# Dense expert ups moved ahead of the last product stage: 39 to 47, with the last six tied behind the one-hot products

## The chip, the cores and the metric

The kernel runs on one core of one Trainium2 chip. The metric is the device time of one execution, in microseconds (us). Three runs of the kernel before gave a median of 1912.57 us (1909.86 to 1913.16). An execution was recorded by the hardware profiler; all durations below come from that record.

The core has engines that run side by side, each in its own fixed order: TensorE (PE in the profile, its weight loads PEld), VectorE (DVE), ScalarE (ACT), GpSimd (POOL) and SyncE (SP), which here only issues DMA transfers. An instruction that waits holds up everything behind it on its own engine.

## The reference, cut to what matters

The block maps `x` of 512 tokens by 1024 features to the same shape: an attention branch and a recurrent branch, merged and added to `x`, and then a retrieval of experts (PEER), the part that matters here:

```python
def peer_ffn(h, w_q, sub_keys, u_tab, v_tab):      # per block of 128 tokens
    q = (hb @ w_q).reshape(PEER_BLOCK, PEER_HEADS, 2, PEER_HALF)
    sc = jnp.einsum('thcd,hcnd->thcn', q, sub_keys)
    s1, i1 = lax.top_k(sc[:, :, 0], 16); s2, i2 = lax.top_k(sc[:, :, 1], 16)
    ...                                            # 16 best of the 256 sums: idx, g = softmax
    act = jax.nn.gelu(jnp.einsum('thkd,td->thk', u_tab[idx], hb))
    return jnp.einsum('thk,thkd->td', g * act, v_tab[idx])
```

Each token picks 16 of 16384 experts in each of 8 heads, 128 picks in all. An expert is one row of `u_tab` and one of `v_tab`, of 1024 floats each.

## The kernel before, in words

The tokens are four blocks of 128. Pass `p0` holds block 0, pass `p1` blocks 1 to 3. The trunk (attention, recurrence, merge, projection) runs for `p0` and then for `p1`. The experts are computed in two ways.

**By gather** (`experts`, blocks 0 and 1): 128 slots, one for each pick. For a slot, POOL issues an indirect DMA (L848) that gathers 128 rows of `uv`, 1 MB, into one of 4 buffers. DVE multiplies the u half with `h2` and sums (L855, tile `uv`), ACT makes the weight `e` (L860, L861), and DVE adds the weighted v half to the running sum (L838, tile `x1g`). Block 0's slots run next to the trunk of `p1`, block 1's next to the dense part below. A gather has a manual dependency on an instruction of the step that it was recorded in, called its turn: in the last stage `turn[0]` is that step's multiplication `o` on DVE (L1028). How many slots a step records is set by `SHARE`: 0.2 for an up next to the search, 0.5 for a group of one-hot products, 0.6 for a product alone, 1.1 for a product with an up.

**Densely** (blocks 2 and 3, 256 tokens): all 16384 experts in 128 chunks of 128.

- *Up* (`up`): the chunk's u rows times the 256 tokens, then a gelu (L917) into a result `y`. The first 39 chunks (`AHEAD`) are made ahead, in plain float32, 8 products of 16 PE instructions in all, from `p1.h2r`, with no work on DVE. The other 89 are made inside the last stage, split in two fp32r terms each: ACT casts (L899), DVE subtracts (L900), and PE does 24 products (tile `st`).
- *Search* (`topk`): DVE finds the picks. `ups_far` puts 26 ups (`LEAD`) on PE next to it (tile `pup`).
- *One-hot products* (`wbuild`): the picks of blocks 2 and 3 become a dense table of weights, 16 groups of 16 tokens. Each group is 16 small products (tile `pw`, L1003), copied by ACT to `wst` and stored to `w_d` in HBM. Here 13 further ups run.
- *Last stage* (`down`): for each chunk DVE multiplies `y` with its weights, read back from `w_d`, into `o` (L1028, three buffers, `OB`), and PE adds `o` times the chunk's v rows to `acc`: 8 instructions of 512 columns. From chunk 24 on an up goes with each product. `run(ex)` at the end takes what slots are left.

The code records instructions in program order; a scheduler with a timeline of its own then sets the order on every engine. So an engine's order need not be the code's. Sync dependencies made with `add_manual_dep` hold in any order.

Of the kernel before, what the change touches and what calls it, by code (L numbers as in the profile page):

```python
# [9 lines left out]
F32 = mybir.dt.float32  # L10
F32R = mybir.dt.float32r
# [4 lines left out]
ALU = mybir.AluOpType  # L16
AX = mybir.AxisListType

P = 128
D = 1024  # L20
KT = D // P
# [41 lines left out]
def block_kernel(  # L63
# [17 lines left out]
    nc = tc.nc  # L81
    V = nc.vector
# [6 lines left out]
    pp = ctx.enter_context(tc.tile_pool(name="pp", bufs=2))  # L89
    dram = ctx.enter_context(tc.tile_pool(name="dram", bufs=1, space=bass.MemoryType.DRAM))  # L90
    wp = ctx.enter_context(tc.tile_pool(name="wp", bufs=4))
    ap = ctx.enter_context(tc.tile_pool(name="ap", bufs=1))
    rg = ctx.enter_context(tc.tile_pool(name="rg", bufs=5))
    trunk = ctx.enter_context(ExitStack())
    s4 = trunk.enter_context(tc.tile_pool(name="s4", bufs=2, side="right"))
    s2 = trunk.enter_context(tc.tile_pool(name="s2", bufs=5, side="right"))

# [107 lines left out]

    def mm(o, lhs, rhs, start, stop):
        terms = [(0, 0)] if len(lhs) == 1 or len(rhs) == 1 else [(0, 0), (0, 1), (1, 0)]
        for i, (a, b) in enumerate(terms):
            nc.tensor.matmul(  # L209
                o, lhs[a], rhs[b], start=start and i == 0, stop=stop and i == len(terms) - 1  # L210
            )


    in_turn = mybir.DependencyInfo(mybir.DependencyClass.Sync, mybir.DependencyReason.SCHED_ONLY)
# [665 lines left out]
    NG = NT2 // TG  # L880
    NCH = SLOTS

    HEAD, MID = 24, 15
    AHEAD = HEAD + MID

    TURN = list(range(HEAD, AHEAD)) + list(range(HEAD)) + list(range(AHEAD, SLOTS))

    LEAD = 26

    WI = 12  # L890

# [9 lines left out]
        return t[:, 0, :], t[:, 1, :]  # L901


    def up(c, S_):
        ks = lambda k: slice(k * P, (k + 1) * P)
        if c < AHEAD:
            u = wp.tile([P, D], F32, tag="raw", name=nm("u"), bufs=3)
            nc.sync.dma_start(u, u_t[c])
            for k in range(KT):
                mm(S_, [u[:, ks(k)]], [p1.h2r[:, k, :]], k == 0, k == KT - 1)  # L910
        else:
            uhi, ulo = chunk(u_t, c, "near")
            for k in range(KT):
                mm(S_, [uhi[:, ks(k)], ulo[:, ks(k)]], [h[:, k, P : 3 * P] for h in p1.h2T], k == 0, k == KT - 1)

    def gelu(o, S_):
        return A.activation(o, S_, AF.Gelu_apprx_tanh)  # L917
# [26 lines left out]


    def kept(c):
        if c >= HEAD:
            return mid.tile([P, NT2], F32, tag="ym", name=nm("y"), bufs=MID)
        if c % WI == 0:
            ybuf.append(rg.tile([P, WI, NT2], F32, tag="r", name=nm("ys")))  # L950
        return ybuf[-1][:, c % WI, :]
# [12 lines left out]
    def dense(ys, kT, kTb, stack):  # L964
# [3 lines left out]
        pt_ = pool("pt", 2, space=PSUM)  # L968
        acc = pa.tile([P, 2, D], F32, tag="acc", name="acc")

        def up_near():
            c = TURN[len(ys)]
            st = pt_.tile([P, 512], F32, tag="st", name=nm("st"))
            up(c, st[:, 0:NT2])
            y = kept(c)
            gelu(y, st[:, 0:NT2])
            ys[c] = y


        def wbuild(tg):  # L980
            o1s = wp.tile([P, TG, P], F32, tag="w8", name=nm("o1s"))
            st = wp.tile([P, NCH, TG], F32, tag="w8", name=nm("wst"))
            for t4 in range(0, TG, 4):
                pw = pt_.tile([P, 4, P], F32, tag="pw", name=nm("pw"))
                t0_ = tg * TG + t4
                o2 = dw.tile([P, 4, P], F32, tag="o2", name=nm("o2"), bufs=4)
                V.tensor_tensor(  # L987
                    o2, iota.unsqueeze(1).to_broadcast([P, 4, P]),
                    kTb[:, t0_ : t0_ + 4].unsqueeze(2).to_broadcast([P, 4, P]), op=ALU.is_equal,
                )  # L990
                for j in range(4):
                    t = t0_ + j
                    o1 = o1s[:, t4 + j, :]
                    k1, g1 = kT[:, 0, 0, t : t + 1], kT[:, 0, 1, t : t + 1]
                    if O1[j] == "A":

                        sq = dw.tile([P, P], F32, tag="osq", name=nm("osq"), bufs=2)
                        A.activation(sq, iota, AF.Square, bias=kT[:, 1, 0, t : t + 1])
                        A.activation(o1, sq, AF.Relu, scale=kT[:, 1, 1, t : t + 1], bias=g1)
                    else:  # L1000
                        e = nc.gpsimd if O1[j] == "P" else V
                        e.tensor_scalar(o1, iota, k1, g1, op0=ALU.is_equal, op1=ALU.mult)  # L1002
                    nc.tensor.matmul(pw[:, j, :], o2[:, j, :], o1, start=True, stop=True)  # L1003
                turn[0] = A.copy(st[:, :, t4 : t4 + 4], pw.rearrange("p t i -> p i t"))  # L1004
            nc.sync.dma_start(w_d[tg], st)

        ws, vs = [], []

# [24 lines left out]
                    mm(acc[:, b, hs], [o[:, bs]], [v_[:, hs]], c == 0, c == NCH - 1)  # L1033

        for tg in range(NG):
            wbuild(tg)
            share("w")
            if len(ys) < AHEAD - 6:
                up_near()

            if tg == 7:
                wtile()
                wload(0, 0, 8)
            elif tg == 13:
                wload(0, 8, 14)
        wload(0, 14, NG)
        while len(ys) < AHEAD:
            up_near()
        for c in range(NCH):
            down(c, ys[c])  # L1050
            if c >= HEAD and len(ys) < NCH:
# [9 lines left out]
    st = {}  # L1061
# [10 lines left out]
    p1.rnn()  # L1072
    p1.merge()
    p1.project()
    trunk.close()
    mid = ctx.enter_context(tc.tile_pool(name="mid", bufs=1, reuse_waits="tile", side="right"))
    run(p1.keys())
    when = []
    for name, mark in marks:
        owed[0] += PACE[name]  # L1080
# [12 lines left out]
        yield from experts(P, x1, h2, (p1.idx[:, 0, :], p1.g[:, 0, :]), lambda s: turn[0], True)  # L1093

    ex = second()
    ys = ups_far(0, LEAD)
    p1.weights()
    kTs = picks_t()
# [86 lines left out]
```

## Time and profile before

| what | value |
|---|---|
| median of three runs | 1912.57 us |
| the profiled execution | 1909.11 us, of which the traced span is 1907.2 us |
| PE busy | 1750.3 us, 92% of the span |
| DVE busy | 1310.4 us, 69% |
| ACT busy, POOL busy | 783.9 us, 41%; 486.7 us, 26% |
| search with ups | 942 to 1050 us of the span |
| one-hot products | 1052 to 1180 us |
| last stage | 1200 to 1901 us |

A busy share is an average over stages, so each stage has to be read by itself: which engine has no gaps there, and what ended the gaps of the others. Names in the trace are tile names of the program without their numbers; "out<-in" says what an instruction writes and reads. A value in square brackets behind a row is the idle time before it and what ended it.

### The profile page before, as it was taken

The page shows a single profiled execution, that of the slowest core. Times are in us where ns is not written, and L with a number is a line of the kernel's source. Part 1 is how long each engine was busy: PE and PEld are TensorE (multiplying, and loading weights), DVE is VectorE, ACT ScalarE, POOL GpSimd, SP SyncE. Part 2 cuts the span into 40 slices and gives each one's busy share as a digit, 9 for nine tenths or more (in the row PEclk, how much of TensorE's full clock was granted, in tenths as well). Part 3 has the DMA queues.
Part 4 walks back from the last instruction along what each step waited for, and adds up shares of the span by engine and source line. Part 5 has one row for each costly group of instructions (what it writes and reads, how often), then busy time and mean ns, then how long its engine had stood idle before and what let it go on. Part 6 is the DMA issues. An engine that isn't in the chain of part 4 may idle for free.

```text
span 1907.2 us, 25762 instructions
## 1 busy us (share of the span) xinstructions
PE 1750.3 (92%) x9166; PEld 1378.6 (72%) x9166; DVE 1310.4 (69%) x2818; ACT 783.9 (41%) x2193; POOL 486.7 (26%) x375
## 2 busy tenths in 40 slices
PE   7899898888798899989996985899999999999998
PEld 6789797778598677779985885347766767667763
DVE  2251387988889987689999567456666666666662
ACT  3382333767678754355311565012222322232220
POOL 1100001545322233342001466122222232222220
PEclk9899897889599899999998998899999999999999
DMA  7488454887877899987464577999999999999893
GB/s 296 149 279 309 172 193 162 297 293 283 308 274 278 313 389 357 386 305 271 155 216 157 177 275 290 362 372 395 366 369 392 382 354 364 354 356 354 331 359 123
DMA packets 131471, 563.37 MB, mean 295 GB/s; under 512 B 11408, under 2 KB 43280, under 8 KB 88592
## 3 DMA queue, kind: packets, MB, share of 16 engines
q1 hardware_dynamic: 94480, 293.29, 42.8%
q0 software_dynamic: 36864, 268.45, 37.0%
q8 instruction: 72, 1.18, 0.2%
q14 instruction: 55, 0.45, 0.1%
HBM read 539.68 MB, written 22.02 MB: 295 GB/s over the span
## 4 chain that ended last, share of the span: by engine, by line
PE 71%; DVE 11%; DMA 9%; ACT 5%; issue 3%; POOL 1%; DVEq 0%; SPq 0%; ACTq 0%; POOLq 0%
PE acc L209 22%; PE st L209 16%; DMA uv<-in_uv_dram,idx 6%; PE ppq L209 5%; PE pkq L209 5%; PE pgt L209 4%; PE pbR L684 4%; PE pbA L677 3%; PE pwo L711 2%; DVE x1f L838 2%; PE pw L1003 2%; PE pvv L209 1%; DMA w_d<-wst 1%; DVE uv L855 1%; DMA v<-in_v_t_dram 1%
## 5 line engine op out<-in xcount | busy, mean ns | idle before, releaser
L848 POOL DMA_INDIRECT uv<-in_uv_dram,idx x256 | 360.4, 1408 | 1075.8 <-DVE x1g L838 284.3
L209 PE MATMUL acc<-v,o 128*128 128x512 f32 x1024 | 449.9, 595 | 22.2 <-DVE o L1028 19.6
L209 PEld LDWEIGHTS acc<-v,o 128*128 128x128 f32 x1024 | 191.8, 191 | 246.5 <-issue 223.3
L209 PE MATMUL st<-a,t 128*128 128x256 f32 x2136 | 282.2, 292 | 0.0
L209 PEld LDWEIGHTS st<-a,t 128*128 128x128 f32 x2136 | 262.5, 191 | 22.2 <-issue 18.9
L838 DVE SCALAR_TENSOR_TENSOR x1g<-uv,e,x1g 128x1024 f32<-128x1024 f32 x128 | 164.3, 1283 | 52.8 <-ACT e L861 52.8
L838 DVE SCALAR_TENSOR_TENSOR x1f<-uv,e,x1f 128x1024 f32<-128x1024 f32 x128 | 164.0, 1281 | 24.9 <-ACT e L870 24.8
L855 DVE SCALAR_TENSOR_TENSOR uv<-uv,h2f 128x1024 f32<-128x1024 f32 x128 | 156.0, 1220 | 34.5 <-DMA uv<-in_uv_dram,idx 27.9
L855 DVE SCALAR_TENSOR_TENSOR uv<-uv,h2g 128x1024 f32<-128x1024 f32 x128 | 155.9, 1218 | 19.4 <-DMA uv<-in_uv_dram,idx 19.4
L860 ACT ACTIVATE e<-e 128x1 f32<-128x1 f32 x128 | 25.8, 202 | 333.7 <-DVE uv L855 333.4
L900 DVE TENSOR_TENSOR t<-raw,t 128x1024 fp32r<-128x1024 f32 x89 | 108.9, 1223 | 68.7 <-ACT t L899 68.7
L1028 DVE TENSOR_TENSOR o<-y,w 128x256 f32<-128x256 f32 x104 | 44.0, 424 | 102.9 <-PE acc L209 102.9
L917 ACT ACTIVATE y<-st 128x256 f32<-128x256 f32 x89 | 34.2, 384 | 193.5 <-PE st L209 193.5
L230 DVE TENSOR_TENSOR wl<-raw,wh 128x1024 fp32r<-128x1024 f32 x76 | 90.8, 1218 | 19.0 <-ACT wh L229 7.3
L899 ACT CAST t<-raw 128x1024 fp32r<-128x1024 f32 x89 | 92.0, 1033 | 23.4 <-PE acc L209 23.4
L229 ACT CAST wh<-raw 128x1024 fp32r<-128x1024 f32 x76 | 76.7, 1046 | 35.0 <-PE pwo L711 12.3
L209 PE MATMUL pup<-r,u 128*128 128x256 f32 x416 | 90.4, 379 | 0.1
L209 PEld LDWEIGHTS pup<-r,u 128*128 128x128 f32 x416 | 78.8, 190 | 11.1 <-issue 0.5
L1003 PE MATMUL pw<-o1s,o 128*128 128x128 f32 x512 | 70.8, 295 | 15.0 <-DVE o L987 9.8
L1002 POOL TENSOR_SCALAR o1s<-iota,r 128x128 f32<-128x128 bf16 x64 | 74.2, 1168 | 38.3 <-ACT r L928 16.3
L1003 PEld LDWEIGHTS pw<-o1s,o 128*128 128x128 f32 x512 | 66.6, 206 | 20.0 <-ACT wst L1004 9.0
L209 PE MATMUL pkq<-wh,a 128*128 128x256 f32 x384 | 78.5, 298 | 0.0
(264 smaller groups left out, 3251.1 us busy)
## 6 DMA issues: line engine op xcount, KB each, us to landing
v<-in_v_t_dram SPq DMA_DIRECT2D x64, 1024.0 KB
raw<-in_u_t_dram SPq DMA_DIRECT2D x89, 512.0 KB
u<-in_u_t_dram SPq DMA_DIRECT2D x39, 512.0 KB
w<-in_w_br_dram SPq DMA_DIRECT2D x16, 1024.0 KB
w_d<-wst SPq DMA_DIRECT2D x16, 1024.0 KB
w<-w_d SPq DMA_DIRECT2D x9, 1536.0 KB
w<-in_w_qkv_dram SPq DMA_DIRECT2D x12, 1024.0 KB
raw<-in_w_qkv_dram SPq DMA_DIRECT2D x24, 512.0 KB
```

The source lines that it names most:

```text
L209: nc.tensor.matmul(o, lhs[a], rhs[b], start=start and i == 0, stop=stop and i == len(terms) - 1)
L229: A.copy(hi[:, i : i + 1024], raw)
L230: V.tensor_tensor(lo[:, i : i + 1024], raw, hi[:, i : i + 1024].bitcast(F32), op=ALU.subtract)
L677: nc.tensor.matmul(pb[:, 0:NT], w.raw(k * P, (k + 1) * P), self.aT[:, k, :], start=(k == 0), stop=(k == H - 1))
L684: nc.tensor.matmul(pb[:, 0:NT], w.raw(1024 + k * P, 1024 + (k + 1) * P), self.rnn_out(k, 1)[:, 0, :], start=(k == 0), stop=(k == NF - 1),)
L838: V.scalar_tensor_tensor(x1, v_, e_, x1, op0=ALU.mult, op1=ALU.add)
L848: i = nc.gpsimd.indirect_dma_start(out=t, out_offset=None, in_=uv, in_offset=bass.IndirectOffsetOnAxis(ap=idx[:, s : s + 1], axis=0),)
L855: i = V.scalar_tensor_tensor(t[:, 0:D], t[:, 0:D], 1.0, h2, op0=ALU.mult, op1=ALU.mult, accum_out=d)
L899: A.copy(t[:, 0, :], raw)
L900: V.tensor_tensor(t[:, 1, :], raw, t[:, 0, :].bitcast(F32), op=ALU.subtract)
L1002: e.tensor_scalar(o1, iota, k1, g1, op0=ALU.is_equal, op1=ALU.mult)
L1003: nc.tensor.matmul(pw[:, j, :], o2[:, j, :], o1, start=True, stop=True)
```

## The change

It makes 47 ups ahead in place of 39, and 81 in the last stage in place of 89. Of the 47, 31 are recorded next to the search (26 before), 10 between the one-hot products (7 before), and 6 behind them, as before. New is that the first product of each of these six has a dependency on the last one-hot product, so that the scheduler cannot put them earlier. The eight more results lie in a tile `spare`, and two tiles `h2s` hold the split token operand for the ups of the last stage, made by one cast on ACT and one subtraction on DVE. Both take the place in SBUF of the keys' operand buffer (pool `ap`), which is now freed with the trunk, after the keys. The share per step is untouched; the sums of the shares shift since there are fewer steps with an up.

```diff
-    ap = ctx.enter_context(tc.tile_pool(name="ap", bufs=1))
...
+    ap = trunk.enter_context(tc.tile_pool(name="ap", bufs=1, side="right"))
...
-    HEAD, MID = 24, 15
-    AHEAD = HEAD + MID
+    HEAD, MID, SPARE = 24, 15, 8
+    AHEAD = HEAD + MID + SPARE
-    LEAD = 26
+    LEAD, HELD = 31, 6
...
-    def up(c, S_):
+    def up(c, S_, after=None):
...
-                mm(S_, [u[:, ks(k)]], [p1.h2r[:, k, :]], k == 0, k == KT - 1)
+                i = mm(S_, [u[:, ks(k)]], [p1.h2r[:, k, :]], k == 0, k == KT - 1)
+                if after is not None and k == 0:
+                    tc.add_manual_dep(i.ins, after.ins.name, in_turn, reason="in turn")
...
-                mm(S_, [uhi[:, ks(k)], ulo[:, ks(k)]], [h[:, k, P : 3 * P] for h in p1.h2T], k == 0, k == KT - 1)
+                mm(S_, [uhi[:, ks(k)], ulo[:, ks(k)]], [h[:, k, :] for h in h2s], k == 0, k == KT - 1)
...
-            if len(ys) < AHEAD - 6:
+            if len(ys) < AHEAD - HELD:
                 up_near()
...
         while len(ys) < AHEAD:
-            up_near()
+            up_near(last)
+
+        A.copy(h2s[0], p1.h2r)
+        V.tensor_tensor(h2s[1], p1.h2r, h2s[0].bitcast(F32), op=ALU.subtract)
...
+    run(p1.keys())
     trunk.close()
     mid = ctx.enter_context(tc.tile_pool(name="mid", bufs=1, reuse_waits="tile", side="right"))
-    run(p1.keys())
...
+    h2s = [mid.tile([P, KT, NT2], F32R, tag=f"h{i}", name=f"h2s{i}") for i in range(2)]
+    spare = mid.tile([P, SPARE, NT2], F32, tag="spare", name="spare")
```

What the scheduler makes of it shows in the order on the engines. First PE, where the one-hot products (`pw`) end and the last stage (`acc`) begins; `x4` counts products, `st` is an up. Before:

```order
L1003 MATMUL pw_10354<-o1s_10338,o_2090_10355 128x128 x4
L1003 MATMUL pw_10368<-o1s_10338,o_2093_10369 128x128 x4
L1003 MATMUL pw_10382<-o1s_10338,o_2096_10383 128x128 x4
L209 MATMUL acc<-v_10479,o_10481 128x512 x4
L209 MATMUL acc<-v_10479,o_10487 128x512 x4
L209 MATMUL acc<-v_10500,o_10502 128x512 x4
```

And now, at the same place on PE:

```order
L1011 MATMUL pw_10475<-o1s_10445,o_2111_10476 128x128 x4
L1011 MATMUL pw_10489<-o1s_10445,o_2114_10490 128x128 x4
L209 MATMUL st_10512<-r_6202,u_10513 128x256 x8
L209 MATMUL st_10524<-r_6202,u_10525 128x256 x8
L209 MATMUL st_10536<-r_6202,u_10537 128x256 x8
L209 MATMUL st_10548<-r_6202,u_10549 128x256 x8
L209 MATMUL st_10560<-r_6202,u_10561 128x256 x8
L209 MATMUL acc<-v_10588,o_10590 128x512 x3
L209 MATMUL st_10572<-r_6202,u_10573 128x256 x8
L209 MATMUL acc<-v_10588,o_10590 128x512
```

Five of the six tied ups stand between the last one-hot product and the first product of the last stage, the sixth inside that first product.

Second DVE, in the middle of the last stage, around products 59 to 64. The last number in a name grows in the order in which the code records; so a slot `uv` belongs to the `o` whose number is next below its own, and that `o` is its gather's turn. Before:

```order
L1028 TENSOR_TENSOR o_2452_12392<-y_2339_11723,w_2271_11308 128x256
L900 TENSOR_TENSOR t_2455_12401<-raw_2454_12399,t_2455_12401 128x1024
L838 SCALAR_TENSOR_TENSOR x1g_8972<-uv_2433_12286,e_2434_12288,x1g_8972 128x1024
L855 SCALAR_TENSOR_TENSOR uv_2440_12331,e_2441_12333<-uv_2440_12331,h2g_8973 128x1024
L1028 TENSOR_TENSOR o_2461_12441<-y_2346_11768,w_2366_11876 128x256
L838 SCALAR_TENSOR_TENSOR x1g_8972<-uv_2440_12331,e_2441_12333,x1g_8972 128x1024
L900 TENSOR_TENSOR t_2464_12450<-raw_2463_12448,t_2464_12450 128x1024
L855 SCALAR_TENSOR_TENSOR uv_2442_12338,e_2443_12340<-uv_2442_12338,h2g_8973 128x1024
L1028 TENSOR_TENSOR o_2468_12486<-y_2354_11815,w_2366_11876 128x256
L838 SCALAR_TENSOR_TENSOR x1g_8972<-uv_2442_12338,e_2443_12340,x1g_8972 128x1024
L855 SCALAR_TENSOR_TENSOR uv_2450_12385,e_2451_12387<-uv_2450_12385,h2g_8973 128x1024
L1028 TENSOR_TENSOR o_2476_12533<-y_2361_11860,w_2366_11876 128x256
```

Now, in the same stretch on DVE:

```order
L1037 TENSOR_TENSOR o_2486_12595<-y_2312_11556,w_2384_11985 128x256
L1037 TENSOR_TENSOR o_2494_12642<-y_2319_11601,w_2384_11985 128x256
L904 TENSOR_TENSOR t_2466_12465<-raw_2465_12463,t_2466_12465 128x1024
L858 SCALAR_TENSOR_TENSOR uv_2491_12633,e_2492_12635<-uv_2491_12633,h2g_8977 128x1024
L904 TENSOR_TENSOR t_2473_12510<-raw_2472_12508,t_2473_12510 128x1024
L841 SCALAR_TENSOR_TENSOR x1g_8976<-uv_2491_12633,e_2492_12635,x1g_8976 128x1024
L858 SCALAR_TENSOR_TENSOR uv_2499_12680,e_2500_12682<-uv_2499_12680,h2g_8977 128x1024
L841 SCALAR_TENSOR_TENSOR x1g_8976<-uv_2499_12680,e_2500_12682,x1g_8976 128x1024
L1037 TENSOR_TENSOR o_2501_12687<-y_2327_11648,w_2384_11985 128x256
L1037 TENSOR_TENSOR o_2509_12734<-y_2334_11693,w_2384_11985 128x256
```

Before, the slot uv_2450 (turn: the `o` ahead of o_2452) stood behind three more multiplications, o_2452, o_2461 and o_2468. Now two `o` stand together, and the two slots behind them, uv_2491 (turn o_2486) and uv_2499 (turn o_2494), have their turns one and none back. From slot 52 on (product 45) all slots up to 121 stand so, in place of two or three `o` back before; every tenth product has a third slot in its pair.

## Rows read from the trace of the kernel before

**Rows 1.** Stretches: length, busy PE, PEld, DVE, ACT, POOL; PEclk, DMA share, GB/s.
```profile
310.00:540.00 230.00, 195.71 (x1152) 169.88 (x1153) 192.58 (x302) 148.47 (x503) 98.92 (x65) 0.81 0.76 277
540.00:660.00 120.00, 106.41 (x517) 94.26 (x516) 116.49 (x163) 99.64 (x249) 29.94 (x23) 0.94 0.86 308
1200.00:1300.00 100.00, 97.44 (x254) 45.88 (x255) 48.66 (x73) 10.82 (x31) 22.05 (x17) 0.98 1.02 380
1300.00:1500.00 200.00, 200.00 (x1024) 139.92 (x1023) 136.58 (x173) 59.48 (x139) 49.26 (x36) 1.00 0.98 379
```
**Rows 2.** Chain that ended last, in order of time, inside the last stage.
```profile
1350.88 5.75 PE st L209 x48
1356.63 6.87 PE acc L209 x16
```
**Rows 3.** Groups of the last stage: busy, mean ns | idle before, releasers.
```profile
L209 PE MATMUL acc<-v,o 128*128 128x512 f32 x1024 | 449.9, 595 | 22.2 <-DVE o L1028 19.6 <-DMA v<-in_v_t_dram 2.6
L848 POOL DMA_INDIRECT uv<-in_uv_dram,idx x115 | 163.7, 1424 | 512.0 <-DVE x1g L838 284.3 <-DVE o L1028 222.5 <-issue 5.2
L855 DVE SCALAR_TENSOR_TENSOR uv<-uv,h2g 128x1024 f32<-128x1024 f32 x115 | 140.1, 1218 | 0.0
L900 DVE TENSOR_TENSOR t<-raw,t 128x1024 fp32r<-128x1024 f32 x89 | 108.9, 1223 | 68.7 <-ACT t L899 68.7
```
**Rows 4.** Groups of the search: the ups beside it.
```profile
L209 PE MATMUL pup<-r,u 128*128 128x256 f32 x416 | 90.4, 379 | 0.1
```
**Rows 5.** Timeline at the search's end: start, us, engine, line [idle before].
```profile
1044.55 0.87 PE L925 MATMUL pt<-ident,r 128*128 128x128 f32 x3 [12.81 <-DVE r L320]
1050.69 0.90 PE L925 MATMUL pt<-ident,r 128*128 128x128 f32 x3 [5.27 <-DVE r L320]
```
**Rows 6.** Timeline of PE over the one-hot products.
```profile
1051.87 3.37 PE L1003 MATMUL pw<-o1s,o 128*128 128x128 f32 x16 [0.27 <-DVE o L987]
...
1116.60 3.19 PE L209 MATMUL st<-r,u 128*128 128x256 f32 x14
1119.62 8.76 PE L1003 MATMUL pw<-o1s,o 128*128 128x128 f32 x64
...
1173.91 6.41 PE L1003 MATMUL pw<-o1s,o 128*128 128x128 f32 x40 [1.26 <-ACT wst L1004]
1199.94 5.26 PE L209 MATMUL acc<-v,o 128*128 128x512 f32 x6 [19.62 <-DVE o L1028]
```
**Rows 7.** Timeline of the last gather, its turn and its slot.
```profile
1856.01 0.43 DVE L1028 TENSOR_TENSOR o<-y,w 128x256 f32<-128x256 f32 x1 [3.01 <-PE acc L209]
1856.70 1.67 POOL L848 DMA_INDIRECT uv<-in_uv_dram,idx  x1 [2.50 <-DVE o L1028]
...
1870.08 1.22 DVE L855 SCALAR_TENSOR_TENSOR uv<-uv,h2g 128x1024 f32<-128x1024 f32 x1
1871.91 1.28 DVE L838 SCALAR_TENSOR_TENSOR x1g<-uv,e,x1g 128x1024 f32<-128x1024 f32 x1 [0.60 <-ACT e L861]
1873.18 0.43 DVE L1028 TENSOR_TENSOR o<-y,w 128x256 f32<-128x256 f32 x1
```
**Rows 8.** Two gathers issued together, and the slots that waited for them.
```profile
346.57 1.45 POOL L848 DMA_INDIRECT uv<-in_uv_dram,idx  x1 [0.20 <-DVE x1f L838]
348.32 1.99 POOL L848 DMA_INDIRECT uv<-in_uv_dram,idx  x1 [0.30 <-DVE r L465]
...
352.63 1.22 DVE L855 SCALAR_TENSOR_TENSOR uv<-uv,h2f 128x1024 f32<-128x1024 f32 x1 [0.86 <-DMA uv<-in_uv_dram,idx]
355.92 1.23 DVE L855 SCALAR_TENSOR_TENSOR uv<-uv,h2f 128x1024 f32<-128x1024 f32 x1 [0.52 <-DMA uv<-in_uv_dram,idx]
```
**Rows 9.** Chain in order of time: two more gathers that were waited for.
```profile
513.34 6.48 DMA uv<-in_uv_dram,idx
1135.59 10.94 DMA uv<-in_uv_dram,idx
```
**Rows 10.** Waits of DVE: for what, us in total, times, longest us.
```profile
DVE uv L855 <- DMA uv<-in_uv_dram,idx: 47.3, 33, 9.4
```

More of the change, by code (lines that the diff above doesn't have):

```diff
@@ L207, in mm @@
         terms = [(0, 0)] if len(lhs) == 1 or len(rhs) == 1 else [(0, 0), (0, 1), (1, 0)]
-        for i, (a, b) in enumerate(terms):
+        made = [
             nc.tensor.matmul(
@@ L211, in mm @@
             )
+            for i, (a, b) in enumerate(terms)
+        ]
+        return made[0]
     in_turn = mybir.DependencyInfo(mybir.DependencyClass.Sync, mybir.DependencyReason.SCHED_ONLY)
@@ L946, in kept @@
     def kept(c):
+        if HEAD + MID <= c < AHEAD:
+            return spare[:, c - HEAD - MID, :]
         if c >= HEAD:
@@ L969, in dense, with up_near @@
         acc = pa.tile([P, 2, D], F32, tag="acc", name="acc")
-        def up_near():
+        def up_near(after=None):
             c = TURN[len(ys)]
             st = pt_.tile([P, 512], F32, tag="st", name=nm("st"))
-            up(c, st[:, 0:NT2])
+            up(c, st[:, 0:NT2], after)
             y = kept(c)
@@ L1002, in wbuild @@
                         e.tensor_scalar(o1, iota, k1, g1, op0=ALU.is_equal, op1=ALU.mult)
-                    nc.tensor.matmul(pw[:, j, :], o2[:, j, :], o1, start=True, stop=True)
+                    last = nc.tensor.matmul(pw[:, j, :], o2[:, j, :], o1, start=True, stop=True)
                 turn[0] = A.copy(st[:, :, t4 : t4 + 4], pw.rearrange("p t i -> p i t"))
             nc.sync.dma_start(w_d[tg], st)
+            return last
         ws, vs = [], []
@@ L1035, in dense @@
         for tg in range(NG):
-            wbuild(tg)
+            last = wbuild(tg)
             share("w")
-            if len(ys) < AHEAD - 6:
+            if len(ys) < AHEAD - HELD:
                 up_near()
```

## The prediction

> **What bounds the kernel now.** I read the busy times by stage first, then the chain that ended last, then the waits and the timeline at the places that the change touches.
>
> In the last stage PE has no gap: 200.00 us busy of 200.00 at full granted clock [rows 1]. The chain agrees: two ups take 5.75 us, two products 6.87 us, and so on to the end [rows 2]. A near up is thus 2.87 us, a product 3.43 us, and a pair of each 12.62 us. DMA runs close behind, at a share of 0.98 and 379 GB/s [rows 1], but PE waited only 2.6 us for v in the whole stage, and the slots' first DVE step (L855) not at all for its gather: 0.0 idle before its 115 instructions [rows 3]. In the search DVE is the bound; PE ends its 26 ups (90.4 us, 3.48 each) [rows 4] and then idles 12.81 and 5.27 us [rows 5]. Over the one-hot products PE is full while ups stand between them, up to 1119.62; the rest takes until 1180.32, and then PE idles 19.62 us for the stores to `w_d` and their way back [rows 6].
>
> So what PE does in the last stage counts in full, and what it does beside the search or in that gap should cost little. What can turn this round is whatever makes PE wait in the last stage: `o` from DVE.
>
> **Ups taken out of the last stage.** 89 become 81: 8 x 2.87 = 23.0 us less. Their casts (ACT) and subtractions (DVE, 1.22 us each [rows 3]) go too, but neither engine bounds this stage now.
>
> **Ups put in ahead.** Five more beside the search are 5 x 3.48 = 17.4 us, and the idle there is 12.81 + 5.27 = 18.1 us: hidden, though without that cover they would cost all of it. The subtraction for `h2s` covers 2048 elements, two of the 1.22 us kind, 2.44 us on DVE, which bounds the search; between 0 and 2.44 I take the upper end. Between the one-hot products there are 10 ups in place of 13. Before, 1051.87 to 1119.62 held 13 ups (45.2 us) and 96 one-hot products (the other 22.5 us, 0.235 each), and the remaining 160 took 60.7 us, 0.38 each [rows 6]. Now 64 stand among the ups and 192 follow: 10 x 3.48 + 64 x 0.235 + 192 x 0.38 = 123 us for 128 before, so the last one is about 5.6 - 2.4 = 3.2 us earlier. Five tied ups (17.4 us) fit the gap of 19.62 us. The sixth stands inside the first product: 3.5 us in full. Three u loads and three raw loads, 3.1 MB, now come when the last stage starts, where DMA already has a share of 1.02 at 380 GB/s [rows 1]: between 0 and 3.1 MB / 380 GB/s = 8 us; I take 0, since PE's wait for v there was 2.6 us in all and the sixth up gives v 3.5 us more. Sum of this paragraph: about 0, between -4 and +10.
>
> **The new order on DVE.** This is the term that decides. A gather waits for its turn, the `o` of its step. The trace shows it: `o` at 1856.01 (product 117, counted back from the last), gather at 1856.70, 0.69 us later, released by that `o`; its slot began at 1870.08, 13.4 us after the gather, four `o` on [rows 7]. In the middle of the stage the slots stood two or three `o` behind their turn, two to three times 6.3 us, and none waited [rows 3]. Now from product 45 to 104 two `o` come together and the two slots of these turns follow at once. DVE must stand and wait for a transfer that the `o` just ahead of it has released.
>
> How long does a gather take from issue to use? Where a slot waited for it, the row gives it: 352.63 - 346.57 = 6.06 us for the first of two issued 1.75 us apart, 355.92 - 348.32 = 7.60 for the second [rows 8]; single ones 6.48 and 10.94 [rows 9]. DVE had 33 such waits in all [rows 10]; these rows hold the shortest and, to 0.02 us, the longest. In the last stage two are issued together beside v and raw loads, so I take 8.0, and keep 6.1 and 10.9 as bounds.
>
> By the Trainium skill, "DMA: Bandwidth & Descriptors", section "Anatomy of one DMA — SWDGE (gpsimd) path", a DMA from GpSimd takes about 2.0 us and its bytes at 436 GB/s: an estimate of 4.4 us for 1 MB. The rows do not agree: the shortest is 6.06 us, with other transfers on the same engines. By the page's figure a pair would take 7.4 + 4.4 = 11.8 us, under PE's 12.62, and the wait would be hidden.
>
> A pair's cycle on DVE, from the first `o` to the next first `o`: 0.69 us to the gather, 8.0 to land, then slot A 1.2, a subtraction 1.2, x1g of A 1.2, slot B to its x1g 1.83, x1g to the next `o` 1.27 (both from rows 7: 1870.08, 1871.91, 1873.18) [rows 7]. The second gather is issued about 1.75 us after the first, and lands while A is worked on. The sum is 7.4 + 8.0 = 15.4 us, against 12.62 on PE: 2.8 us more for each of 30 pairs, 84 us. Six of these pairs hold a third slot, another 1.2 + 1.2 less 0.6 of the wait for `e` that it fills: 6 x 1.8 = 11 us. Against it stands a lead: with three buffers `o` may be ahead by two products and two pairs of ups, 2 x 3.43 + 4 x 2.87 = 18 us, which DVE loses before PE feels anything.
>
> After product 104 PE has only products left. Five slots there stand none or one `o` behind their turn, and each costs 0.69 + 8.0 + 1.83 + 1.27 + 0.4 = 12.2 us in a row, 61 us for products 104 to 111 and the last two ups, which take PE 8 x 3.43 + 5.75 = 33 us: 28 more. The next three are two `o` behind and cost nothing; three more, one behind, take 10.3 us (no x1g in the chain) for two products of 6.87: 10 more. Together 38.
>
> **Sum.** -23 + 0 + 84 + 11 - 18 + 38 = +92 us. The profiled execution took 1909.1 us (its span and 1.9 around it), 3.5 below the median, which I leave out: 2001, and I predict 2000 us. At 6.1 us for a gather the terms are 13.5 a pair, 26 + 11 - 18 + 23 - 23 = +19, 1928. At 10.9 us 18.3 a pair, 170 + 11 - 18 + 61 - 23 = +201, 2110.
>
> **Rivals.**
>
> *The gathers land in time.* If a gather took 5.2 us or less, the pair would stay at 12.62, the tail would lose little, and what is left is the 23 us: 1909 - 23 = 1886, faster. For it: PE-bound now, five of six ups in a true gap, and with DVE waiting fewer bytes are in flight. Against it: not one waited gather below 6.06 us, with DMA at 277 or 308 GB/s [rows 1, 8, 9], and a pair of 15.4 us still asks 379 x 12.62 / 15.4 = 311 GB/s. The point from which it decides is 5.2 us; at 5.6 or so gain and loss cancel, and the time is as before.
>
> *DMA gets worse in bursts.* The two gathers (2 MB), a v load and raw loads are now released within a few us of each other and then DMA drains. That speaks for 10 us and more for each: 2075 to 2110. Against it: DVE's wait lowers the mean rate, and the second of a pair took 7.60 us [rows 8].
>
> *PE's clock falls in the gaps.* PE would be busy 12.62 of 15.4 us, 82%; from 310 to 540, at 85%, the granted clock was 0.81 [rows 1]. A pair would then take PE 12.62 / 0.81 = 15.6 us, just over DVE's 15.4: some 30 x 0.2 = 6 us more, 2007. It hides behind the same wait and hardly moves the sum.
>
> *The ups don't fill the gap.* If the late u loads or the stores to `w_d` hold each other up, the first product comes up to 10 us later: 2010, inside the range. By the order they are in place.
>
> **Chances.** The DVE wait at 6.1 us and above, up to some 9.5: 0.73; longer gathers: 0.15; the gathers in time: 0.09; gain and loss about equal: 0.03. About 0.2%, 4 us, is what can be told from no change here. Slower 0.88, same 0.03, faster 0.09. The range from 1915 to 2075 leaves out the faster case and the worst of the bursts, a tenth at either end; 1930 to 2050 is the likeliest case's own.
>
> **What would show it.** Right: in the last stage L855's rows (now L858) wait for `uv<-in_uv_dram,idx`, 2 to 5 us each from product 45 on; POOL's gathers are released by `o` in nearly every step; PE's products wait for `o`; the pair of products and ups comes every 15 us in the chain; GB/s there falls to about 310; the first product starts near 1197 us, with five ups in the gap before it. Wrong: slots still without a wait, a gather used 5 us after issue, or the last stage at 12.6 us a pair. If the pair takes 13 or 18 us, the mechanism holds and the gather's time was mis-sized.

## The result, and the profile after

The changed kernel takes 2215.18 us (median of four runs, 2211.71 to 2220.13), the kernel before 1911.21 in the same comparison: a ratio of 1.159, 95% interval 1.156 to 1.162. Slower was forecast, but 2000 us and at most 2075. The loss is more than three times the forecast one (304 us by the medians, where the sum gave 92), and its mechanism is another, so that even the direction came out right for the wrong reason.

First, where the time is. The rows of `o` give it: product 45, product 105 and the last product. The kernel before:

```profile
1410.56 0.42 DVE L1028 TENSOR_TENSOR o<-y,w 128x256 f32<-128x256 f32 x1 [0.86 <-PE acc L209]
...
1788.96 0.42 DVE L1028 TENSOR_TENSOR o<-y,w 128x256 f32<-128x256 f32 x1 [0.86 <-PE acc L209]
...
1890.34 0.43 DVE L1028 TENSOR_TENSOR o<-y,w 128x256 f32<-128x256 f32 x1 [3.01 <-PE acc L209]
```

The same three products of the changed kernel:

```profile
1408.35 0.42 DVE L1037 TENSOR_TENSOR o<-spare,w 128x256 f32<-128x256 f32 x1
...
2094.29 0.42 DVE L1037 TENSOR_TENSOR o<-y,w 128x256 f32<-128x256 f32 x1 [8.92 <-PE acc L209]
...
2201.48 0.42 DVE L1037 TENSOR_TENSOR o<-y,w 128x256 f32<-128x256 f32 x1 [2.72 <-PE acc L209]
```

Up to product 45 the new kernel is 2.2 us ahead. From there to product 105, 30 pairs, it takes 685.9 us in place of 378.4, so 22.9 us a pair in place of 12.6. That is 307.5 of the 311 us. The last 22 products take 107.2 us and took 101.4.

Second, which engine has gaps there. Two stretches of the last stage after (length, busy PE, PEld, DVE, ACT, POOL; PEclk, DMA share, GB/s), the first to be read against the last of [rows 1]:

```profile
1300.00:1500.00 200.00, 161.59 (x743) 105.66 (x742) 117.83 (x149) 46.52 (x111) 39.27 (x30) 0.90 0.81 309
1500.00:1700.00 200.00, 127.35 (x557) 82.31 (x556) 77.39 (x95) 34.15 (x75) 17.80 (x19) 0.79 0.57 206
```

PE had no gap in that stretch before. Now it is idle for more than a third of the second stretch, its granted clock is 0.79, and the DMA share is 0.57. No engine is the bound any more, so the stage is a loop of waits. The groups say what is waited for (busy, mean ns | idle before, releasers):

```profile
L209 PE MATMUL acc<-v,o 128*128 128x512 f32 x1024 | 523.8, 674 | 256.0 <-DMA v<-in_v_t_dram 256.0
L1037 DVE TENSOR_TENSOR o<-y,w 128x256 f32<-128x256 f32 x96 | 40.8, 425 | 390.3 <-PE acc L209 390.3
L858 DVE SCALAR_TENSOR_TENSOR uv<-uv,h2g 128x1024 f32<-128x1024 f32 x128 | 156.5, 1222 | 94.4 <-DMA uv<-in_uv_dram,idx 94.0
L923 ACT ACTIVATE y<-st 128x256 f32<-128x256 f32 x81 | 30.8, 381 | 364.5 <-DVE o L1037 333.3
```

The last of these groups in the kernel before:

```profile
L917 ACT ACTIVATE y<-st 128x256 f32<-128x256 f32 x89 | 34.2, 384 | 193.5 <-PE st L209 193.5
```

Against [rows 3], PE's wait for v grew from 2.6 to 256.0 us. The wait of DVE for gathers, on which the prediction rests, is the smallest of the four (94.0 us, of which 77.8 lie in the last stage). The Gelus have a releaser that they did not have before: there those of the last stage waited for their own sums on PE (193.5 us), never for an `o`.

Third, one pair in order of time (start, us, engine, line [idle before]; `...` stands for rows left out; a row "x2" merges two and runs from the start of the first to the end of the last; SPq is SyncE's queue, on which DMA transfers are issued):

```profile
1519.73 0.43 DVE L1037 TENSOR_TENSOR o<-y,w 128x256 f32<-128x256 f32 x1 [9.54 <-PE acc L209]
...
1520.19 0.38 ACT L923 ACTIVATE y<-st 128x256 f32<-128x256 f32 x1 [11.32 <-DVE o L1037]
...
1520.43 0.94 POOL L851 DMA_INDIRECT uv<-in_uv_dram,idx  x1 [19.11 <-DVE o L1037]
...
1522.56 6.21 PE L209 MATMUL st<-h2s,t 128*128 128x256 f32 x48
...
1523.16 1.05 ACT L903 CAST t<-raw 128x1024 fp32r<-128x1024 f32 x1 [2.59 <-PE acc L209]
...
1525.50 3.29 SPq L901 DMA_DIRECT2D raw<-in_u_t_dram  x2
...
1526.06 1.22 DVE L858 SCALAR_TENSOR_TENSOR uv<-uv,h2g 128x1024 f32<-128x1024 f32 x1 [0.59 <-DMA uv<-in_uv_dram,idx]
...
1527.21 1.22 DVE L904 TENSOR_TENSOR t<-raw,t 128x1024 fp32r<-128x1024 f32 x1
...
1528.88 0.39 SPq L1033 DMA_DIRECT2D v<-in_v_t_dram  x1
...
1536.77 8.79 PE L209 MATMUL acc<-v,o 128*128 128x512 f32 x13 [8.00 <-DMA v<-in_v_t_dram]
...
1543.45 0.42 DVE L1037 TENSOR_TENSOR o<-y,w 128x256 f32<-128x256 f32 x1 [10.80 <-PE acc L209]
```

Read it as a loop. The `o` at 1519.73 releases the Gelu (0.46 us later). The two ups (`st`) then run right behind the products, and end at 1522.56 + 6.21 = 1528.77. Only 0.11 us later is v issued for the next two products. PE can use it 7.9 us after that and stands idle until then; the first products then run at half the clock; and only they let the next `o` be made. A pair is products, ups and a whole v load, one after the other. (Two loads of u stand ahead of v on the queue, and they are out at 1525.50 + 3.29 = 1528.79. So this trace alone doesn't say whether v waits for them or for the ups; experiments 9 and 15 do.)

In the kernel before v went out much earlier, for a pair in the middle 18.2 us before the product that uses it (1577.96 and 1596.12), with the ups and products of the pair ahead still to come on PE:

```profile
1577.96 1.22 SPq L1024 DMA_DIRECT2D v<-in_v_t_dram  x1
```
```profile
1596.12 7.03 PE L209 MATMUL acc<-v,o 128*128 128x512 f32 x16
```

Over the pairs from product 48 to 103 the median is 18.2 us before and 7.7 now.

Counted over the last stage, the `o` at 1519.73 is that of product 55, and the Gelu it releases is that of chunk 70. The same count for all 81: the first 15 Gelus inside the last stage come 20 to 23 products ahead, every later one (from chunk 62, near product 47) exactly 15. Fifteen is the number of buffers that near results take in turn (`MID`). In the kernel before the count was mostly 13 or 14 (12 to 15), and no Gelu waited for an `o`.

Why it binds now is in the code. The ups inside the last stage start at product 24 with the first chunk not made ahead: 39 before, so 15 steps ahead of use, 47 now, so 23 ahead. But the eight `spare` places serve once, for chunks 39 to 46, and all later results share the 15 others. So a near up is recorded eight steps before a buffer for its result can be free.

Last, the stretch between the one-hot products and the first product, which answers to [rows 6]:

```profile
1171.66 2.96 PE L1011 MATMUL pw<-o1s,o 128*128 128x128 f32 x24 [1.28 <-DVE o L995]
1174.46 10.53 PE L209 MATMUL st<-r,u 128*128 128x256 f32 x48
1192.85 9.68 PE L209 MATMUL st<-r,u 128*128 128x256 f32 x32 [7.86 <-DMA u<-in_u_t_dram]
1202.36 2.74 PE L209 MATMUL acc<-v,o 128*128 128x512 f32 x6
```

The gap of 19.62 us before the first product is mostly filled, but PE waits 7.86 us inside it for the u of a tied up. The first product comes 2.4 us later than before; forecast was 3 us earlier.

### The profile page after: what moved, and what is told of

Read it like the earlier page. It is cut to its first block, busy times and chain, and to the rows that moved or that the text cites. A ratio compares the mean times of both kernels' runs of the same rounds, so it can differ in the third digit from the quotient of the medians.

```text
span 2218.3 us, 25677 instructions
## 1 busy us (share of the span) xinstructions
PE 1825.7 (82%) x9102; PEld 1399.2 (63%) x9102; DVE 1313.5 (59%) x2811; ACT 789.1 (36%) x2188; POOL 448.7 (20%) x375
## 4 chain that ended last, share of the span: by engine, by line
issue 40%; PE 31%; DVE 9%; DMA 8%; POOL 8%; ACT 4%; POOLq 0%; DVEq 0%; SPq 0%; ACTq 0%
POOL uv L851 7%; PE acc L209 6%; DMA uv<-in_uv_dram,idx 5%; PE ppq L209 4%; PE pkq L209 4%; PE st L209 3%; DMA v<-in_v_t_dram 2%; PE pry L209 2%; PE prx L209 2%; PE pup L209 1%; PE pvv L209 1%; PE pw L1011 1%; DVE x1f L841 1%; PE pgt L209 1%; DVE uv L858 1%
## 5 line engine op out<-in xcount | busy, mean ns | idle before, releaser
L209 PE MATMUL acc<-v,o 128*128 128x512 f32 x1024 | 523.8, 674 | 256.0 <-DMA v<-in_v_t_dram 256.0
L851 POOL DMA_INDIRECT uv<-in_uv_dram,idx x256 | 317.0, 1238 | 1459.7 <-DVE o L1037 781.4
L209 PEld LDWEIGHTS acc<-v,o 128*128 128x128 f32 x1024 | 219.1, 219 | 531.8 <-issue 278.1
L209 PE MATMUL st<-h2s,t 128*128 128x256 f32 x1944 | 252.4, 288 | 0.0
L209 PEld LDWEIGHTS st<-h2s,t 128*128 128x128 f32 x1944 | 234.3, 188 | 20.4 <-issue 20.1
L858 DVE SCALAR_TENSOR_TENSOR uv<-uv,h2g 128x1024 f32<-128x1024 f32 x128 | 156.5, 1222 | 94.4 <-DMA uv<-in_uv_dram,idx 94.0
L841 DVE SCALAR_TENSOR_TENSOR x1f<-uv,e,x1f 128x1024 f32<-128x1024 f32 x128 | 163.8, 1280 | 22.9 <-ACT e L873 22.8
L903 ACT CAST t<-raw 128x1024 fp32r<-128x1024 f32 x81 | 84.9, 1048 | 146.9 <-PE acc L209 98.9
L904 DVE TENSOR_TENSOR t<-raw,t 128x1024 fp32r<-128x1024 f32 x81 | 99.1, 1224 | 43.4 <-ACT t L903 43.2
L209 PE MATMUL pup<-r,u 128*128 128x256 f32 x496 | 107.9, 379 | 1.5 <-DMA u<-in_u_t_dram 1.5
L209 PEld LDWEIGHTS pup<-r,u 128*128 128x128 f32 x496 | 93.8, 190 | 14.9 <-issue 2.4
L233 DVE TENSOR_TENSOR wl<-raw,wh 128x1024 fp32r<-128x1024 f32 x76 | 90.7, 1217 | 18.3 <-ACT wh L232 6.6
L1010 POOL TENSOR_SCALAR o1s<-iota,r 128x128 f32<-128x128 bf16 x64 | 79.8, 1255 | 20.5 <-PE pw L1011 7.9
L209 PE MATMUL pgt<-a,wh 128*128 128x384 f32 x256 | 70.9, 357 | 5.1 <-DVE r L627 5.1
```

The lines of the kernel that those rows point to most:

```text
L209: nc.tensor.matmul(o, lhs[a], rhs[b], start=start and i == 0, stop=stop and i == len(terms) - 1)
L233: V.tensor_tensor(lo[:, i : i + 1024], raw, hi[:, i : i + 1024].bitcast(F32), op=ALU.subtract)
L841: V.scalar_tensor_tensor(x1, v_, e_, x1, op0=ALU.mult, op1=ALU.add)
L851: i = nc.gpsimd.indirect_dma_start(out=t, out_offset=None, in_=uv, in_offset=bass.IndirectOffsetOnAxis(ap=idx[:, s : s + 1], axis=0),)
L858: i = V.scalar_tensor_tensor(t[:, 0:D], t[:, 0:D], 1.0, h2, op0=ALU.mult, op1=ALU.mult, accum_out=d)
L903: A.copy(t[:, 0, :], raw)
```

## The experiments

Theories: **G**, the prediction's (DVE waits for gathers asked for late); **R** (the ring of 15 buffers); **S** (v stands on SyncE's queue behind loads of u); **T** (the tie, the copied operands or the 47 themselves). **W** came later: v waits for one of four weight buffers.

**1. All 23 buffers in one rotation.**

```diff
     def kept(c):
-        if HEAD + MID <= c < AHEAD:
-            return spare[:, c - HEAD - MID, :]
         if c >= HEAD:
-            return mid.tile([P, NT2], F32, tag="ym", name=nm("y"), bufs=MID)
+            return mid.tile([P, NT2], F32, tag="ym", name=nm("y"), bufs=MID + SPARE)
...
-    spare = mid.tile([P, SPARE, NT2], F32, tag="spare", name="spare")
```

> Still 47 ahead, but the near up products' results take 23 buffers in rotation (the 15 and the eight spare ones together) instead of 15. In the changed kernel an up product is written 23 steps ahead of its use but its result's buffer is freed only 15 steps ahead, so that its Gelu waits for an o (333.3 us over 34 waits on ScalarE, none before). Theory R (the ring of 15): with 23 buffers no Gelu waits for an o, the pair of products takes about 12.6 us again instead of 23.7, and the kernel takes 1888 us (1875 to 1905). Rival T (the tied products, the copied operands or the 47 themselves cost the time): 2215 us as now, within 15.

Measured: 1885.77 us, ratio to before 0.988 (0.985 to 0.991). The stretch of the last stage and the groups of that kernel:

```profile
1500.00:1700.00 200.00, 200.00 (x1023) 138.76 (x1023) 133.35 (x170) 57.64 (x134) 47.84 (x35) 1.00 0.95 363
```
```profile
L209 PE MATMUL acc<-v,o 128*128 128x512 f32 x1024 | 446.9, 592 | 2.0 <-DMA v<-in_v_t_dram 2.0
L858 DVE SCALAR_TENSOR_TENSOR uv<-uv,h2g 128x1024 f32<-128x1024 f32 x114 | 138.9, 1218 | 15.8 <-DMA uv<-in_uv_dram,idx 15.8
L923 ACT ACTIVATE y<-st 128x256 f32<-128x256 f32 x81 | 31.0, 383 | 152.9 <-PE st L209 152.8
```

No Gelu waits for an `o` (they come 20 to 23 products ahead to the end), PE is full at full clock, and on DVE the slots stand two or three `o` behind their turns again. R holds, T falls; the order on DVE was itself a result of the ring.

**2. The near ups begin eight steps later**, with 15 buffers and the spare ones as they were.

```diff
-            if c >= HEAD and len(ys) < NCH:
+            if c >= HEAD + SPARE and len(ys) < NCH:
                 up_near()
-            share("both" if c >= HEAD and len(ys) < NCH else "down")
+            share("both" if c >= HEAD + SPARE and len(ys) < NCH else "down")
```

> Still 47 ahead with 15 buffers and the eight spare ones, but the near up products begin eight steps later, at product 32 instead of 24, so that each is written 15 steps ahead of its use, as in the kernel before. Theory R: no Gelu waits for an o, 12.6 us a pair, 1888 us (1875 to 1905). Rival T: 2215 us within 15.

Measured: 1887.41 us, ratio 0.989 (0.986 to 0.991), and again no Gelu waits for an `o`. It is not the number of buffers but the number against the lead.

**3. No gathers in the last stage.** `for s in range(14 if table else SLOTS)` in `experts`: this leaves out 114 of the 128 slots of block 1, so its outputs are not computed.

> The changed kernel with the second block's slots left out from the fifteenth on (114 gathers, their turns on VectorE and their sums; these outputs are not computed), so no gather runs beside the last stage. Theory G, the prediction's (VectorE waits for gathers that are asked for late): without them the pair falls to 13 us or less and the kernel takes under 1920 us. Theories R and S (S: the v load stands on SyncE's queue behind the loads of u, which wait for VectorE's subtractions, and so comes 8 us late): the Gelu's wait for an o and PE's wait for v stay, the pair takes 18 us or more, and the kernel over 2040 us.

Measured: 2137.74 us, 20.5 us a pair (median between products, as in all that follow). The loop in its bare form:

```profile
1522.31 6.22 PE L209 MATMUL st<-h2s,t 128*128 128x256 f32 x48
...
1528.56 0.38 SPq L1033 DMA_DIRECT2D v<-in_v_t_dram  x1
...
1534.30 9.02 PE L209 MATMUL acc<-v,o 128*128 128x512 f32 x16 [5.77 <-DMA v<-in_v_t_dram]
```

G falls: without one gather beside it the pair still takes 20.5 us of 23.4. v is issued at the end of the ups (1522.31 + 6.22 = 1528.53). What the gathers add is mostly v's landing: from its issue to PE's use of it the median is 7.7 us beside them and 5.9 alone.

**4. Each v load written one pair earlier in the code.**

```diff
             if c % 2 == 0:
-                vs.append(wp.tile([P, 2, D], F32, tag="w8", name=nm("v")))
-                nc.sync.dma_start(vs[-1], v_t[c : c + 2].rearrange("c p d -> p c d"))
-            v_ = vs[-1][:, c % 2, :]
+                for n in range(c, min(c + 4, NCH), 2):
+                    if n // 2 == len(vs):
+                        vs.append(wp.tile([P, 2, D], F32, tag="w8", name=nm("v")))
+                        nc.sync.dma_start(vs[-1], v_t[n : n + 2].rearrange("c p d -> p c d"))
+            v_ = vs[c // 2][:, c % 2, :]
```

> The changed kernel with each v load written one pair of products earlier, so that on SyncE's queue it stands two loads of u further ahead; the Gelus still wait for an o, and the slots' turns stand 0 or 1 o behind their gathers on VectorE as in the changed kernel. Theory S: PE no longer waits 8 us for v in each pair, the pair falls to 16 us or less, and the kernel takes 1985 us or less. Theory G: unchanged, 2215 within 30. Theory R alone (the wait of the Gelu for an o closes a loop through the casts, whichever load comes last): 2100 to 2215.

Measured: 2083.80 us, 19.0 us a pair; better than R alone allowed, far worse than S. Here v is issued at the start of the ups, and still comes too late (median 9.6 us to its use, of which PE stands 4.0):

```profile
1506.49 6.22 PE L209 MATMUL st<-h2s,t 128*128 128x256 f32 x48
1507.09 0.38 SPq L1035 DMA_DIRECT2D v<-in_v_t_dram  x1
```

**5. The loop without the 47:** `HEAD, MID, SPARE = 24, 7, 8`, `LEAD = 26`, so 39 ahead.

> 39 up products ahead as in the kernel before, but eight of their results in the spare buffers and only 7 buffers in rotation for the near ones, which are still written 15 steps ahead: the same eight steps too early as in the changed kernel, without its 47. Theory R: Gelus wait for o from about product 31 on, the v loads come behind the loads of u, some 38 pairs at 20 to 24 us instead of 12.6, and the kernel takes 2230 to 2340 us, worse than with 47 ahead, since more near products are left. Rival T (the 47 cost the time): 1911 within 20.

Measured: 2333.84 us, 23.0 us a pair, slower than with 47 ahead, as R said. Its Gelus:

```profile
L923 ACT ACTIVATE y<-st 128x256 f32<-128x256 f32 x89 | 33.9, 381 | 445.1 <-DVE o L1037 428.3
```

**6 and 7. Six and four steps too early** (`SPARE = 6`, `LEAD = 29`; `SPARE = 4`, `LEAD = 28`; the tile `spare` keeps its size, here and in experiment 8).

> The changed kernel with six spare buffers and 45 ahead: near up products six steps too early for their 15 buffers. On VectorE the slots' turns stand 0 or 1 o behind their gathers as in the changed kernel, but on SyncE's queue v stands two loads of u further ahead. Theory S (with R): like the kernel with the earlier v load, about 17 us a pair, 2050 to 2120 us. Theory G (the slots' turns alone): 2200 to 2240.

> The changed kernel with four spare buffers and 43 ahead: four steps too early. The two up products whose sums wait in PSUM and the one in its weights take up about three of these steps, so theory R expects few waits of a Gelu for an o (under 100 us) and 1900 to 1960 us; a loss in proportion to the steps (six pairs of eight for six, four of eight for four) would give 2060.

Measured: 2083.67 us with six (19.8 us a pair; the Gelus waited 207.1 us for `o`), 1908.56 with four (12.5; 72.3 us). So it is no loss per step. With four, too, every Gelu from chunk 58 on comes exactly 15 products ahead, but v still goes out 14.5 us before its use (median), and PE waits only 9.8 us for it in all: a Gelu that waits is not yet a slow pair. It isn't free either: the last stage has four ups fewer than before (11.5 us) and takes 710.1 us, 2.9 more than before, so some 14 us are lost in single pairs. The six agree with S in the total but not in the pair (S had about 17), and S falls in experiment 9.

**8. The other parts of the change with 39 ahead:** `SPARE = 0`, `LEAD = 26`.

> 39 ahead and 15 buffers as before, with the other parts of the change: the second operands copied behind the search, the pool moved, the six last up products tied behind the last one-hot product. Theory R: these cost a few us at most, 1905 to 1920 us, ratio 0.997 to 1.005. Rival T: a loss of 10 us or more.

Measured: 1901.07 us, ratio 0.995 (0.993 to 0.997). They gain a little, more than expected: the first product begins at 1189.93 us, 10.0 earlier than before, with the last stage as long as before (707.2 us both times).

**9. The loads of u on ScalarE's queue:** `nc.scalar.dma_start(raw, src[c])` for the near chunks.

> The changed kernel with the near products' loads of u issued from ScalarE's queue instead of SyncE's, so that no v load stands behind a load of u; the order on VectorE, the 15 buffers and the Gelus' waits for an o stay. Theory S: v is then asked for as soon as its buffer is free, PE's wait for v falls from 8 us to 4 or less a pair, 2040 to 2120 us, as with the earlier v load. If it is not SyncE's queue but only the loop through Gelu, cast and subtraction: 2215 within 30.

Measured: 2228.79 us, 23.2 us a pair: S falls. Two rows of its timeline say why:

```profile
1527.20 6.22 PE L209 MATMUL st<-h2s,t 128*128 128x256 f32 x48
```
```profile
1533.45 0.37 SPq L1033 DMA_DIRECT2D v<-in_v_t_dram  x1
```

No load of u stands ahead of v any more, and v is still issued 0.03 us after the ups end. It waits not for its turn but for a place: v and the split u's take four buffers in turn (tile tag `w8`), and the one that v is to take holds the u of the up just ahead of it on PE. The waits of the queue say the same (us in total, times, longest, from 1500 to 1700 us). In this kernel, and then in the kernel before, where what v waited for most was products, so a place that an earlier v had held:

```profile
SPq L1033 <- PE st L209: 187.6, 9, 23.5
```
```profile
SPq L1024 <- PE acc L209: 42.9, 10, 7.0
```

**10. Experiments 3 and 4 together.**

> The changed kernel with the earlier v load and without the second block's slots from the fifteenth on (their outputs are not computed). A pair took 23.7 us in the changed kernel, 20.4 without the slots, 17.4 with the earlier v load. If the two are separate terms, about 14 us a pair and 1950 to 2000 us; if the v load's landing is all that the slots lengthened, about 16 us and 2010 to 2050.

Measured: 1886.54 us, 12.5 us a pair, lower than either forecast. The terms do not add; it is a race:

```profile
1513.21 6.22 PE L209 MATMUL st<-h2s,t 128*128 128x256 f32 x48
1519.27 7.03 PE L209 MATMUL acc<-v,o 128*128 128x512 f32 x16
```
```profile
1513.81 0.38 SPq L1035 DMA_DIRECT2D v<-in_v_t_dram  x1
```

Issued as the ups begin, v has 5.5 us until PE needs it, and alone it was there in time in 26 of 28 pairs; beside gathers (experiment 4) PE waited in 27 of 28. The Gelus still wait 205.1 us for `o` here, exactly 15 ahead from chunk 62 on; a pair in which v is in time takes 12.5 us all the same.

**11 and 12. The faster kernel of experiment 1, untied** (`up_near()` without `last`), **and with three tied in place of six** (`LEAD, HELD = 34, 3`).

> The kernel with 23 buffers in rotation (1885.8 us, 0.988 of before) with the last six far up products not tied behind the last one-hot product. With the tie the first product of the last stage begins at 1195.96 us after 47 far products, 4.0 earlier than in the kernel before after 39. If the tie fills PE's gap before that product: without it the six stand ahead of the one-hot products they delay, the first product comes 5 to 15 us later, 1891 to 1901 us. If the scheduler's order does without it: 1886 within 3.

> The kernel with 23 buffers in rotation, with 34 up products beside the search instead of 31 and three tied instead of six. PE sits idle for about 23 us of 140 between 1060 and 1200 us in it; if the search has room for three more products (3.4 us of idle time in 120 between 940 and 1060 us speaks against it), the first product of the last stage comes up to 8 us earlier, 1877 to 1884 us; if it has none, they move the search's end and it is 1886 to 1892 us.

Measured, on one chip: untied 1891.16 us, ratio 0.990 (0.989 to 0.992), its first product at 1203.70 us behind a gap of 18.3; three tied 1880.58 us, 0.985 (0.983 to 0.987). With six tied (experiment 1) the first product comes 7.5 us earlier than untied, at 1196.17, but the intervals of the two ratios overlap, so the times alone do not show what six are worth. Three tied are clear of untied, by 10.6 us, though three more ups have moved beside the search there. Their first product is at 1196.89 us, not earlier than in experiment 1, and these two intervals overlap as well: whether three are better than six stays open.

**13 to 15. The wait for the buffer itself.** Three gather buffers in place of four as the control (`uvp`, `bufs=3`); with the space of the fourth a fifth weight buffer (`wp`, `bufs=5`); and that with the loads of u on ScalarE's queue.

> The changed kernel with three buffers for gathered rows instead of four: the control of the two that follow, which spend the 8 KB a partition that this frees. All theories: about as the changed kernel in the last stage, 23 to 25 us a pair; 2215 to 2260 us.

> As the control with three gather buffers, with five weight buffers (for split u's and v together) instead of four. Theory W: v waits for the buffer of the near up product that ends last ahead of it on PE (v is issued 0.1 us after those products end), so it is loaded behind them and not beside them. With a fifth buffer v takes that of the product before, 3.1 us earlier: 18 to 21 us a pair, 80 to 150 us less than the control. Theory S alone (SyncE's queue, v behind the second load of u): within 30 us of the control. If the near up products only run one further ahead with the fifth buffer: within 30 us too, with v still issued at their end.

> The same with five weight buffers, and the loads of u on ScalarE's queue, so that both gates of v are moved, the buffer and the place on SyncE's queue. If both stood 0.3 us apart in the changed kernel (the second load of u issued at 1528.5, the up products' end at 1528.8, v at 1528.88): faster than either alone, 16 to 19 us a pair, 1990 to 2090 us. Theory W alone: as the five buffers alone, within 20 us.

Measured: control 2264.87 us (22.9 us a pair), fifth buffer 2200.61 (21.0), with u on the other queue 2204.34 (20.7). The control is slower than expected ahead of the last stage: its first product is at 1243.58 us in place of 1202.36. The last stages are 1019.5 us long in the control (1016.0 in the changed kernel), 947.5 and 948.8. With five, v goes out in the middle of the ups:

```profile
1703.74 6.22 PE L209 MATMUL st<-h2s,t 128*128 128x256 f32 x48
...
1707.16 1.29 SPq L1033 DMA_DIRECT2D v<-in_v_t_dram  x1
```

That is 3.4 us after they start, when the first of the two ups has ended, and not at their end; without the loads of u on its queue it goes out at the same point. W is shown for the issue of v: one buffer more moves it by one up. The gain, 64 us (72 in the last stage), is under the 80 that I expected as the least, and the place on the queue adds nothing, as W said. These are single runs. Of the other 8 us a pair most is v still: it came 8.6 us after its issue (median) with 2.8 us of ups left to cover it, and PE waited 5.9 us. What would remove that was not tested further.

## Why the prediction was wrong, point by point

**What bounded the kernel before**: right. The last stage is PE's, and in experiment 1 it shrinks with the work: from its first product to the end 1877.4 - 1196.2 = 681.2 us, 707.2 before. That is 26.0 us for eight ups, forecast 23.0.

**The work ahead costs about nothing**: near enough. The first product came at 1202.4, not 1197, and PE waited 7.86 us for a late load of u. That is the cost that I put at 0 between 0 and 8. In experiment 1, with the same ups ahead, PE waited 6.40 us for a u too, but its one-hot products had ended 3.9 us earlier, and the first product came at 1196.2. Against experiment 8, which has the tie without the eight ups, that is 6.2 us later: so much the eight cost ahead of the last stage, and what hid it was the 10.0 us that the other parts gained there. The median of experiment 1, 1885.77, is the 1886 that the prediction gave to its rival "the gathers land in time".

**The new order on DVE, +84 and +11 - 18**: the step that failed. I saw correctly from which product to which the new order runs (45 to 104, 30 pairs), and that the loss begins there. But I took the order as the cause, where it was itself a result of the ring (experiment 1), and gave it the price of a gather: 15.4 us a pair where 22.9 were measured, +77 us where 307.5 were. Experiment 3 takes all gathers away and keeps 20.5 us. What the runs show in its place: a result's buffer that is free 15 products ahead, ups recorded 23 ahead, a Gelu that waits, ups that therefore run just behind a product, their weight buffers held till then, and a v load that can start only after them. That the kernel got slower, as forecast, is luck as far as this step goes. Of the 10.3 us that a pair gained, some 7.7 are PE's wait for v (65.7 us in the 8.5 pairs from 1500 to 1700 us) and some 2.9 are products at the lower clock, 16 times (773 - 592) ns in the same stretch.

I could have seen it ahead of the result. The diff has `mid.tile(..., bufs=MID)` unchanged beside an `AHEAD` grown by `SPARE`. And I took PE's 2.6 us of waiting for v [rows 3] as something that would stay; I never asked which event lets v start, nor how far ahead of its use (18.2 us, a lead that a wait of 2.6 us doesn't show).

**The gather's time, 8.0 us between 6.1 and 10.9**: too long for this kernel, whose DMA share here is 0.57. The gather of the pair shown was issued at 1520.43 and used at 1526.06, 5.6 us later, after a wait of 0.59. Between products 45 and 105, 44 slots waited over 0.2 us for their gather; from issue to use these took 5.3 to 10.0 us, 5.65 in the median. With 5.65 the prediction's own sum gives 13.0 us a pair, 13 us for the 30 pairs in place of 84: even the size of this term came from an oversized gather. By the Trainium skill, "DMA: Bandwidth & Descriptors", section "Anatomy of one DMA — SWDGE (gpsimd) path", a gather of 1 MB would take 4.4 us, an estimate. This trace, at 206 GB/s, comes nearer to that than the rows before did and stays above it.

**The tail, +38**: not borne out, and not measured by itself. With the eight ups taken out (-23) I had +15 behind product 104; the rows give 107.2 - 101.4 = +5.8 behind 105. But the ring changed which work is left there: six ups after product 105 starts (nine before), where in experiment 1, whose ups run 20 to 23 ahead, it is one. There the tail is 78.4 us, 23.0 shorter than before, with no loss.

**Rivals.** "PE's clock falls in the gaps" was right in kind and priced at 6 us: I let PE work through a slow pair, and not stand 8 us for each. "The gathers land in time" is what experiment 1 shows, but only because the order itself went back. None of the four rivals had the ring.

**What would show it**: of my signs, "L855's rows wait 2 to 5 us each" was wrong (77.8 us over 59 waits in the last stage, 1.3 each), and "13 or 18 us a pair means a mis-sized gather" would have led astray: 23 us meant another mechanism. "PE's products wait for `o`" was wrong as well: what they waited for was v.

## What to carry to other kernels

When work is moved ahead by n steps, count for every buffer on its way how many steps ahead that buffer is free; where the lead is larger by more than the steps in between can take up (four too many cost little here, six and eight much), the work isn't early but holds the buffers that later work needs. A stage in which no engine is full, with one wait of a new kind, is a loop: follow it around once in the timeline before pricing any part of it. And a wait "for a DMA" is to be read at that DMA's issue: what ended just before it started is where to look. Here two things did, the loads ahead of it on the queue and the ups that held its buffer, within 0.3 us of each other, and only experiments 9 and 15 tell them apart.

## What the runs showed of the hardware

How long the 1 MB load of v took hung on what ran beside it. With no gathers in the last stage the median of all 64 loads from issue to landing was 5.7 us (experiment 3); in experiment 1, with gathers and DMA at 363 GB/s in the middle of that stage, it was 9.1:

```profile
v<-in_v_t_dram SPq DMA_DIRECT2D x64, 1024.0 KB, 5.7
```
```profile
v<-in_v_t_dram SPq DMA_DIRECT2D x64, 1024.0 KB, 9.1
```

In experiment 1 PE waited 2.0 us for v all the same, since it was issued 18.0 us ahead (median); in the changed kernel, at 206 GB/s, v came 6.7 to 9.1 us after its issue and PE waited for all of it. The load that took longer cost PE less, since it was issued earlier.

Where PE stood idle for 7.8 us in each pair (changed kernel, median) or 5.9 (experiment 3), the granted clock from 1500 to 1700 us was 0.79 and 0.83 on average, and products behind the gap took up to 1222 ns instead of 592, the lower of the two levels (1.2 GHz); in experiment 10, with one such gap of 1.6 us in that stretch, none took over 697, at 1.00.
